# Dealing the projection units anew among the attention quarters, and multiplying by V four quarters at a time

## The chip, the core and the metric

The kernel runs on one core of a Trainium2 chip. The metric is the time of one launch on the device, in microseconds (us), as the median of several runs. Five engines work side by side: TensorE (PE in the profile; its weight loads are PEld), VectorE (DVE), ScalarE (ACT), GpSimd (POOL) and SyncE (SP), which here only issues DMAs.

## What is computed

One layer of an image backbone: 1024 latent tokens of 1024 numbers each, laid out as a grid of 16 rows by 64 columns, and 256 context tokens. Cut to what matters here (the norms, the modulation and the context's own projection are left out):

```python
q, k, v, za, u, bg, cg, zc = jnp.split(h @ w_in, SPLIT_POINTS, axis=-1)   # eight parts of 512 columns
# 8 heads of 64: softmax over a window of 8 x 16 latent keys (with a bias) and all 256 context keys
p = jax.nn.softmax(jnp.concatenate([s_lat, s_ctx], axis=-1), axis=-1)
o = p_lat @ v + p_ctx @ vc
attn = o * jax.nn.silu(za)
conv = bg * centred_short_conv(cg * u, conv_w, conv_b) * jax.nn.silu(zc)
x_new = x + gate[:, None] * (jnp.concatenate([attn, conv], axis=-1) @ w_out)
```

Everything is kept in 32-bit floats. A projection is done as three matmuls of split operands (high times high, high times low, low times high), so each weight tile is first cast into a high part on ACT (tile `uh`) and a low part on DVE (`ul`).

## The kernel before, in words

The program has four stages: the modulation and the norm, up to about 71 us; the projections to q, k and v (up to about 255 us); the attention; and the output projection.

**The attention stage is a loop over quarters.** A quarter is two blocks of 128 latent keys of one head, so a head has four and the loop `quarter(n)` has 32, and three more turns to drain. In this text a quarter's position is n modulo 4. In turn n, PE first transposes running maxima of quarter n-2 (`pmx<-ci,mx`, two small matmuls), then makes the scores of quarter n (`pss`) and the context scores of quarter n+1 (`pc`), and turns the reduced maxima back (`pmx<-ci,rm`). DVE reduces the maxima (`rm<-pmx`), adds up exponentials (`sum<-sum,sb`), adds the bias to the scores of quarter n (`sb<-pss,bt`), subtracts the maxima from quarter n-2 (`sc<-sc,mg` and `sb<-sb,mg`), and folds quarter n into the running maxima (`mx<-pc,sc`, then `mx<-mx,sb`). ACT copies, and takes the exponentials of quarter n-2. All four compute engines run in the order of the code (`strict`); SP's DMAs are not bound to it.

**Multiplying by V.** `weighted` (line 995) multiplies finished exponentials by V into the PSUM tile `po`. Its output is 64 columns wide, and the two halves of `po` (partitions 0 to 63 and 64 to 127) are fed in turn from two lists, sorted by size. Before, it is called in every second turn (o = n-3 even) with two quarters. `total` then sums the exponentials of a finished head (`pmx<-sum,onef`), and `finish` copies both out on ACT (`sums`, `ob`).

**Units and portions.** What is left of the input projection, 16 units of 128 columns, fills PE between these pieces (`unit`, line 369). A unit has two halves of 512 tokens, each with a PSUM bank of tile `pu` (two banks in all), and is cut into 8 portions of six matmuls, four to a half. `TICKS[n]` says how many portions turn n runs: one ahead of `weighted`, the rest behind it. Eight portions run ahead of the loop. Units come in three kinds: the gates of the attention, `attn_group(f)`, whose halves ACT copies to tile `z` and SP stores; and for each group i of the convolution `conv_group(i)`: U and C (tile `ub` on ACT, product `cu` on DVE), its gate z, and G. A convolution's gate keeps both banks until ACT has taken the SiLU of both halves (`zs<-pu`), which is queued when the unit ends and issued at the end of that turn. I write z0 to z3 for the gates of the attention, and U1, C1, zc1, G1 and so on for the groups.

**Chores.** What follows from a unit is queued (`chore`, line 325): ACT's share is issued at the end of the turn (`do_acts`), DVE's share near the start of the next one (`do_dves`), behind the sums and ahead of the bias. A group of the convolution gives DVE two products (`cu`), four taps (`cv<-cu,vecT,cv`), two products with the SiLU (`cv<-zs,cv`) and two with G (`cv<-pu,cv`); a unit gives two `ul`. When a pair of heads is done, `gated(f)` (line 1219 on) loads its row sums and its gate, takes a reciprocal, the SiLU of the gate (`held`, `silus`), and in two later turns multiplies (`zs<-zs,rb`, `tb<-tb,zs`). The exponential and the SiLU need different tables on ACT, so a SiLU costs an ACT_TABLE_LOAD ahead of it and one behind.

**The end.** After the loop the rest of zc3 and G3 runs, and the row sums of the last heads go out and back by DMA to a reciprocal on DVE (`recip`, line 521) that stands ahead of the last `ul` there.

Of the kernel before, what the change touches and what calls it, by code (L numbers as in the profile page):

```python
# [10 lines left out]
F32 = mybir.dt.float32  # L11
# [8 lines left out]
P = 128  # L20
# [7 lines left out]
NPAIR = NH // 2  # L28
# [1 line left out]
CTXT = 3  # L30
FORDER = [4, 5, 6, 0, 1, 2, 3, 7]

TICKS = [2, 3, 3, 3] + 2 * (3 * [4, 2] + [4, 3]) + 6 * [4, 2] + [5, 4, 4]
EPS = 1e-6

LOADS = "x0 x1 x2 x3 s0 c0 s1 c1 x4 x5 x6 x7 t10 t11 s2 t02 t12 c2"
# [19 lines left out]
def body(tc, es, x, xb, xt, cb_, ct, w_mod, w_gate, b_ada, w_grp, w_col, q_g, k_g, bias, w_out, vecs, cst, out):  # L56
# [451 lines left out]
    def attn_group(f):  # L508

        def keep(half, ps):  # L510
            z = cvp.tile([P, 512], F32, name="z", tag="ub", bufs=2)
            act.copy(z, ps)
            sp.dma_start(z_d[f][:, half * 512:(half + 1) * 512], z)

        for got in unit(z_col(f)):
            if got:
                chore(lambda got=got: keep(*got))
            else:
                yield
# [331 lines left out]
    class head:  # L851
# [30 lines left out]
        def ctx_scores(self, g, between=None):  # L882
            pc = psm.tile([P, 2, 256], F32, name="pc", tag="C", bufs=2)
            q = self.q[:, 1, g * 256:(g + 1) * 256]
            for i in range(2):
                if i and between:
                    between()
                for l in range(2):
                    pe.matmul(pc[:, i], self.kc[:, l, i * P:(i + 1) * P], q,
                              start=(i == 0 and l == 0), stop=(i == 1 and l == 1), skip_group_check=True)  # L890
            sc = ap.tile([P, 2, 256], F32, name="sc", tag="sc", bufs=6)
            act.copy(sc, pc)
            self.cps[g] = sc, pc

# [100 lines left out]
    def weighted(quarters):  # L995

        sides = [], []
        for m in quarters:
            for i, hd_, j in pair_of(m):
                if j == 0:  # L1000
                    hd_.po = psm.tile([P, 512], F32, name="po", tag="O", bufs=2)[:]
                for piece in hd_.pieces(j, sbs[m][:, i]):
                    sides[piece[0]].append((hd_, *piece))
            hd_ = heads[m // 4]
            for piece in hd_.ctx_pieces(m % 4):
                sides[piece[0]].append((hd_, *piece))
        for bank, side in enumerate(sides):
            side.sort(key=lambda piece: -piece[-1].free_size())
        for k in range(max(map(len, sides))):
            for bank, side in enumerate(sides):  # L1010
                if k < len(side):
                    hd_, _, j, dst, src = side[k]
                    pe.matmul(dst, hd_.v[:, j], src, start=k == 0 and (hd_, bank) not in opened, stop=k == len(side) - 1,
                              skip_group_check=True)
                    opened.add((hd_, bank))

# [2 lines left out]
    def quarter(n):  # L1019

        live = lambda m: 0 <= m < 4 * NH
        ticks = TICKS[n]
        e, o = n - 2, n - 3
        final = o == 4 * NH - 1
        left = do_frees(1) + 2 if n > 2 else 3
        if live(o):
            heads[o // 4].ctx_sum(o % 4)
        back = maxima(e) if e >= 0 else None
        for m in (o - 1, o)[:1 + final]:
            for i, hd_, j in pair_of(m):  # L1030
                hd_.lat_sum(j, sbs[m][:, i])
        do_dves(left)
        if gating and next(gating[0], "end"):
            gating.pop(0)
        now = pair_of(n)
        for i, hd_, j in now:
            hd_.scores(j, sbank[:, i])
        if n == 0:
            next(fill)
            ticks -= 1  # L1040
        ctx_now = [m for m in ([0, 1] if n == 0 else [n + 1]) if live(m)]
        for m in ctx_now:
            heads[m // 4].ctx_scores(m % 4, back if n >= 2 else None)
        if back and not ctx_now:
            if not now:
                next(fill, None)
                ticks -= 1
            back()

        def biased():  # L1050
            sb = sbs[n] = sb_new()
            bt = now[0][1].bt[:].rearrange("p v n -> p (v n)")[:, :1128].rearrange("p (a n) -> p a n", a=2)
            for at, slot, w_ in (((0, 31, 8), (8, 15, 16)), ((0, 0, 31),), ((0, 0, 31),), ((0, 0, 15), (15, 39, 8)))[n % 4]:
                dve.tensor_tensor(sb[:, :, at * 12:(at + w_) * 12], sbank[:, :, at * 12:(at + w_) * 12],
                                  bt[:, :, slot * 12:(slot + w_) * 12], ALU.add)

        if now and n >= 2:
            biased()
        if live(e):
            heads[e // 4].ctx_exp(e % 4)  # L1060
            w = both(sbs[e], e)
            w4 = w.rearrange("p a (c r) -> p a c r", r=12)
            dve.tensor_tensor(w4, w4, maxima_of(e), ALU.subtract)
            act.activation(w, w, AF.Exp)
        for _ in range(n > 0):
            next(fill, None)
        done = []
        if live(o) and (o % 2 == 0 or final):
            weighted([m for m in ((o - 1, o) if o % 2 == 0 else (o,)) if live(m)])
            if o % 4 == 0 and o or final:  # L1070
                hd_ = heads[(o - 1) // 4]
                pm = back_pm.pop() if not final else psm.tile([P, 512], F32, name="pmx", tag="C", bufs=2)
                hd_.total(pm)
                done.append((hd_, pm))
                if hd_.s:
                    ready.append(hd_.p)
        if now:
            if n < 2:
                biased()
            for m in ctx_now:  # L1080
                heads[m // 4].ctx_max(m % 4)
            for i, hd_, j in now:
                hd_.lat_max(j, sbs[n][:, i])
        back = maxima(-1) if n == 1 else None
        for _ in range(ticks - (n > 0)):
            next(fill, None)
        if back:
            back()
        for hd_, pm in done:
            hd_.finish(pm)  # L1090
        do_acts()
# [3 lines left out]


    def fillers():
        for unit_ in [attn_group(f) for f in range(NPAIR)] + [conv_group(i) for i in range(1, 4)]:
            for got in unit_:
                if got is None:  # L1100
                    yield

    units = [z_col(f) for f in range(NPAIR)]
    for i in range(1, 4):
        units += [CU + i * P, CCG + i * P, z_col(4 + i), CBG + i * P]
    follows.update(zip(units, units[1:]))
    fill = fillers()

# [110 lines left out]
    def gated(f):  # L1219
# [8 lines left out]
        dve.reciprocal(ri, ri)  # L1228
        sp.dma_start(ri_d[f].rearrange("h (x c) -> (h x) c", c=16), ri)
        held.append(zs)  # L1230
        if f:
            chore(lambda: silus(()))
        yield
        while held:
            yield
# [11 lines left out]
    with sbuf("att") as ap, psum("psb") as psb:  # L1247
        sbank = psb.tile([P, 2, 512], F32, name="pss")
        strict[:] = every
        mx = ap.tile([P, T], F32, name="mx")  # L1250
        sb_new = lambda: ap.tile([P, 2, 384], F32, name="sb", tag="sb", bufs=5)
        mg = ap.tile([P, T], F32, name="mg")
        heads[0].load_v()
        for n in range(len(TICKS)):
# [173 lines left out]
```

## Time and profile before

| | us |
|---|---|
| runs: median of three (lowest, highest) | 623.62 (622.5, 623.86) |
| the profiled execution | 622.72 |
| its span, first to last instruction | 620.9 |
| PE busy in the span | 599.6 (97%) |
| DVE, ACT, POOL busy | 399.0, 270.0, 66.9 |
| mean granted PE clock | 0.995 of full speed |

A row of a timeline reads: start, length, engine, line, operation, output <- input, shape, count, and in brackets the idle time of that engine just before and who ended it. Equal neighbours are merged into one row. Nearly every row has line 71, a helper that records operations, so rows are told apart by their tiles. Matmuls overlap, so a row's length is more than its share of the time; starts are the better measure. A row of windows gives, for a stretch that I chose, its length, then for PE, PEld, DVE, ACT and POOL the busy time and the number of instructions, then the granted PE clock, the DMA engines' busy share and GB/s.

### The profile page before, as it was taken

Reading aid. Unit: us, or ns where it says so; the run is one execution under the profiler, and the core shown is the slowest. Engines: PE = TensorE matmul, PEld = TensorE weight load, DVE = VectorE, ACT = ScalarE, POOL = GpSimd, SP = SyncE. Lnnn points to the kernel's source line nnn. Section 1 sums busy time; section 2 is a strip of 40 time slices with the busy share of each in tenths; the row PEclk is TensorE's granted clock in tenths of the full one; section 3 lists DMA queues with packets and bytes.
Section 4 is the critical chain, followed back from the end, with each engine's and each line's share of the span. In section 5 each row is a group of like instructions: output and inputs, shape, how many; then the busy total and the mean of one; then the engine's idle time right before and its main releaser. Section 6 shows DMA issues by size and latency. Waiting matters only on the chain.

```text
span 620.9 us, 9462 instructions
## 1 busy us (share of the span) xinstructions
PE 599.6 (97%) x3348; PEld 502.1 (81%) x3348; DVE 399.0 (64%) x833; ACT 270.0 (43%) x634; POOL 66.9 (11%) x86
## 2 busy tenths in 40 slices
PE   7799999999999999999999999999599999999998
PEld 3577899999999999878787877787378778887887
DVE  1567778556636456577787999879958756484211
ACT  5646354437436364344444373446345425451000
POOL 1001034023223222000000000000000002003300
PEclk9999999999999999999999999999989999999999
DMA  8995567534525674944536364828212316962731
GB/s 324 417 415 185 201 221 216 170 133 145 184 77 170 223 245 153 360 155 177 181 134 233 115 244 137 279 69 297 86 56 86 103 52 204 342 202 99 240 102 51
DMA packets 63226, 116.13 MB, mean 187 GB/s; under 512 B 7377, under 2 KB 26313, under 8 KB 60876
## 3 DMA queue, kind: packets, MB, share of 16 engines
q1 hardware_dynamic: 56684, 103.95, 48.1%
q10 hardware_dynamic: 6240, 11.05, 5.3%
q0 software_dynamic: 256, 0.54, 0.3%
q8 instruction: 26, 0.43, 0.3%
q14 instruction: 20, 0.16, 0.1%
HBM read 86.08 MB, written 29.43 MB: 186 GB/s over the span
## 4 chain that ended last, share of the span: by engine, by line
PE 80%; DVE 8%; DMA 6%; ACT 3%; issue 2%; ACTq 0%; SPq 0%; POOL 0%; DVEq 0%
PE pu L71 26%; PE pacc L71 21%; PE acc L71 5%; PE po L71 4%; PE cacc L71 4%; DMA woraw<-in_w_out 3%; PE pout L90 3%; PE pout L92 3%; PE pout L91 3%; DMA xn<-in_xb 3%; PE pmx L71 3%; PE pss L71 2%; PE pc L71 2%; DVE sb L71 1%; PE tr L71 1%
## 5 line engine op out<-in xcount | busy, mean ns | idle before, releaser
L71 PE MATMUL pu<-h,uh 128*128 128x512 f32 x544 | 172.8, 399 | 7.6 <-ACT zs L71 7.6
L71 PE MATMUL pacc<-w,h 128*128 128x384 f32 x768 | 138.9, 337 | 1.0 <-ACT ub L71 0.6
L71 PEld LDWEIGHTS pacc<-w,h 128*128 128x128 f32 x768 | 132.7, 188 | 1.9 <-ACT ub L71 1.0
L71 PEld LDWEIGHTS pu<-h,uh 128*128 128x128 f32 x544 | 98.9, 190 | 30.8 <-ACT zs L71 8.2
L71 PE MATMUL pu<-h,ul 128*128 128x512 f32 x272 | 107.1, 394 | 0.0
L71 PEld LDWEIGHTS pu<-h,ul 128*128 128x128 f32 x272 | 51.5, 189 | 11.4
L71 POOL TENSOR_TENSOR ss<-ss,few 128x4 f32<-128x4 f32 (+1 forms) x40 | 41.8, 1046 | 125.7 <-DVE ss L71 125.3
L90 PE MATMUL pout<-woh,yh 128*128 128x512 f32 (+2 forms) x136 | 51.6, 380 | 0.1
L91 PE MATMUL pout<-wol,yh 128*128 128x512 f32 (+2 forms) x136 | 51.6, 379 | 0.0
L92 PE MATMUL pout<-woh,yl 128*128 128x512 f32 (+2 forms) x136 | 51.0, 380 | 0.0
L71 ACT ACTIVATE sc<-sc 128x512 f32<-128x512 f32 x32 | 20.2, 632 | 54.4 <-DVE sc L71 54.4
L71 ACT COPY mg<-pmx 128x256 f32<-128x256 f32 (+1 forms) x33 | 12.1, 367 | 66.2 <-PE pmx L71 64.7
L71 DVE TENSOR_REDUCE rm<-pmx 128x2 f32<-128x256 f32 (+1 forms) x33 | 13.7, 416 | 40.3 <-PE pmx L71 40.3
L71 PE MATMUL acc<-h,w 128*128 128x512 f32 x144 | 37.2, 403 | 1.2 <-ACT h L71 1.2
L71 DVE TENSOR_REDUCE ss<-sq 128x4 f32<-128x260 f32 (+1 forms) x40 | 15.7, 393 | 28.6 <-ACT sq L71 27.7
L71 PEld LDWEIGHTS acc<-h,w 128*128 128x128 f32 x144 | 25.8, 188 | 9.3 <-ACT h L71 2.0
L71 DVE TENSOR_TENSOR mx<-mx,sb 128x372 f32<-128x372 f32 (+2 forms) x64 | 31.9, 498 | 1.9
L71 ACT ACTIVATE sq<-pacc 128x256 f32<-128x256 f32 x32 | 12.4, 387 | 47.2 <-PE pacc L71 46.5
L71 DVE TENSOR_TENSOR sum<-sum,sb 128x372 f32<-128x372 f32 (+2 forms) x64 | 31.6, 494 | 1.2
L71 ACT ACTIVATE qn<-pacc,ss 128x64 f32<-128x64 f32 x128 | 30.1, 330 | 4.9 <-PE trA L71 2.5
L90 PEld LDWEIGHTS pout<-woh,yh 128*128 128x128 f32 x136 | 25.6, 188 | 5.3 <-ACT yh L1319 0.6
L92 PEld LDWEIGHTS pout<-woh,yl 128*128 128x128 f32 x136 | 25.6, 188 | 4.8 <-DVE yl L1320 0.2
(141 smaller groups left out, 949.7 us busy)
## 6 DMA issues: line engine op xcount, KB each, us to landing
uraw<-in_w_col SPq DMA_DIRECT2D x34, 256.0 KB
slab<-in_w_mod SPq DMA_DIRECT2D x8, 1024.0 KB
q_d<-qs SPq DMA_DIRECT2D x32, 256.0 KB
k_s<-k_d SPq DMA_DIRECT2D x8, 1024.0 KB
q_s<-q_d SPq DMA_DIRECT2D x16, 512.0 KB
wr<-in_w_grp SPq DMA_DIRECT2D x40, 192.0 KB
bt<-in_rpb SPq DMA_DIRECT2D x8, 564.0 KB
xn<-in_xb SPq DMA_DIRECT2D x8, 512.0 KB
```

Source lines behind the costliest of these rows:

```text
L71: i = emit(*a, **kw)
L90: i = pe.matmul(ps, ah, bh, start=first, stop=False)
L91: pe.matmul(ps, ah, bl, start=False, stop=False)
L92: pe.matmul(ps, al, bh, start=False, stop=last)
```

## The change

Four things. `TICKS` is new: portions still sum to 110 over the 35 turns. The units stand in another order: z0, U1, C1, zc1, G1, z1, U2, C2, zc2, G2, z2, z3, U3, C3, zc3, G3, where before all of z0 to z3 came first. `weighted` is called in every fourth turn with four quarters (and at the end with three), and a first matmul into a bank is now found by the set `opened` alone; two rings of tiles grow from 6 to 8 and from 5 to 7 for it. And the SiLU of the first pair's gate has its own chore, where before it went with that of zc1.

```diff
-TICKS = [2, 3, 3, 3] + 2 * (3 * [4, 2] + [4, 3]) + 6 * [4, 2] + [5, 4, 4]
+TICKS = [2, 3, 3, 3] + 3 * [4, 4, 4, 1] + [4, 4, 4, 2] + 2 * [4, 4, 3, 1] + [4, 4, 2, 1] + [4, 4, 3]
...
-            sc = ap.tile([P, 2, 256], F32, name="sc", tag="sc", bufs=6)
+            sc = ap.tile([P, 2, 256], F32, name="sc", tag="sc", bufs=8)
...
-                    pe.matmul(dst, hd_.v[:, j], src, start=k == 0 and (hd_, bank) not in opened, stop=k == len(side) - 1,
+                    pe.matmul(dst, hd_.v[:, j], src, start=(hd_, bank) not in opened, stop=k == len(side) - 1,
...
-        if live(o) and (o % 2 == 0 or final):
-            weighted([m for m in ((o - 1, o) if o % 2 == 0 else (o,)) if live(m)])
+        if live(o) and (o % 4 == 0 or final):
+            weighted([m for m in range(o - 2 - (o % 4 == 0), o + 1) if live(m)])
...
-        for unit_ in [attn_group(f) for f in range(NPAIR)] + [conv_group(i) for i in range(1, 4)]:
+        for unit_ in (attn_group(0), conv_group(1), attn_group(1), conv_group(2), attn_group(2), attn_group(3), conv_group(3)):
...
-    units = [z_col(f) for f in range(NPAIR)]
+    units = [z_col(0)]
     for i in range(1, 4):
-        units += [CU + i * P, CCG + i * P, z_col(4 + i), CBG + i * P]
+        units += [CU + i * P, CCG + i * P, z_col(4 + i), CBG + i * P] + [z_col(f) for f in ((1,), (2, 3), ())[i - 1]]
...
-        if f:
-            chore(lambda: silus(()))
+        chore(lambda: silus(()))
...
-        sb_new = lambda: ap.tile([P, 2, 384], F32, name="sb", tag="sb", bufs=5)
+        sb_new = lambda: ap.tile([P, 2, 384], F32, name="sb", tag="sb", bufs=7)
```

The portions by turn, counted off the two tables (a unit has portions 0 to 7): before, turn 26 runs zc2.7, G2.0, G2.1, G2.2, so a convolution's gate ends inside a turn. In the changed kernel, turn 7 runs zc1.7 alone (ahead of `weighted`) and turn 8 G1.0 to G1.3; turn 19 runs zc2.6 and zc2.7 and turn 20 G2.0 to G2.3. The ends of C1, C2, zc1, G1, zc2 and G2 lie in turns 5, 17, 7, 9, 19 and 21; they lay in 12, 23, 15, 18, 26 and 28.

On ACT, before, the SiLU of zc2 (turn 26) stands behind that turn's exponentials (`sc`, `sb`) and a table load:

```order
L71 COPY mg<-pmx 128x256
L71 COPY sc<-pc 128x512
L71 ACTIVATE sc<-sc 128x512
L71 ACTIVATE sb<-sb 128x2x288
L71 ACT_TABLE_LOAD
L71 ACTIVATE zs<-pu 128x512 x2
```

In the changed kernel, on ACT at the first such place (zc1, turn 7), the row sums and the output of a head are copied (`sums`, `ob`) between the exponentials and the SiLU:

```order
L71 ACTIVATE sc<-sc 128x512
L71 ACTIVATE sb<-sb 128x2x372
L71 COPY sums<-pmx 128x256
L71 COPY ob<-po 128x512
L71 ACT_TABLE_LOAD
L71 ACTIVATE zs<-pu 128x512 x2
```

So the SiLU on which G waits has moved behind copies that themselves wait for the group by V.

On PE, before, a group of two quarters of one head (turn 5; the tile `v_3052` is V of that head) stands between portions:

```order
L71 MATMUL po<-sb,v_3052 64x23x12
L71 MATMUL po<-sb,v_3052 64x24x12
L71 MATMUL po<-sb,v_3052 64x23x12
L71 MATMUL po<-sb,v_3052 64x24x12
L71 MATMUL po<-sc,v_3052 64x256 x4
L71 MATMUL po<-sb,v_3052 64x7x12
L71 MATMUL po<-sb,v_3052 64x8x12
L71 MATMUL po<-sb,v_3052 64x7x12
L71 MATMUL po<-sb,v_3052 64x8x12
L71 MATMUL pu<-h_164,uh 128x512 x2
```

In the changed kernel, on PE in turn 7, the group of four quarters (three of the first head, V in `v_3055`, and one of the next, `v_3056`) begins so:

```order
L71 MATMUL po<-sb,v_3056 64x24x12
L71 MATMUL po<-sb,v_3055 64x24x12
L71 MATMUL po<-sb,v_3056 64x24x12
L71 MATMUL po<-sb,v_3055 64x24x12
L71 MATMUL po<-sb,v_3055 64x23x12 x4
L71 MATMUL po<-sc,v_3055 64x256 x4
L71 MATMUL po<-sc,v_3056 64x256
```

Pieces of 24 x 12 columns now stand beside pieces of 24 x 12, and those of 23 x 12 beside their like.

On DVE, before, turn 17 holds one `ul` and the two products of `gated` between the sums and the bias:

```order
L71 TENSOR_REDUCE rm<-pmx 128x2
L71 TENSOR_TENSOR sum<-sum,sb 128x31x12 x2
L71 TENSOR_TENSOR ul<-uraw,uh 128x512
L71 TENSOR_TENSOR zs<-zs,rb 128x512
L71 TENSOR_TENSOR tb<-tb,zs 128x512
L71 TENSOR_TENSOR sb<-pss,bt 128x2x372
```

In the changed kernel, turn 17 on DVE holds five chores there:

```order
L71 TENSOR_REDUCE rm<-pmx 128x2
L71 TENSOR_TENSOR sum<-sum,sb 128x31x12 x2
L71 TENSOR_TENSOR ul<-uraw,uh 128x512
L71 TENSOR_TENSOR cu<-pu,ub 128x2x16x16
L71 TENSOR_TENSOR ul<-uraw,uh 128x512
L71 TENSOR_TENSOR zs<-zs,rb 128x512
L71 TENSOR_TENSOR tb<-tb,zs 128x512
L71 TENSOR_TENSOR sb<-pss,bt 128x2x372
```

A second `ul` and a product `cu` came to it, since C2 now ends in this turn.

## The prediction

> **What bounds the kernel now.** I read the page first, then the list of waits, then windows cut at the start of each turn of the attention loop, and last the timelines at the turns that are too long.
>
> ```profile
> span 620.9 us, 9462 instructions
> PE   7799999999999999999999999999599999999998
> PE pu L71 <- ACT zs L71: 7.6, 2, 7.0
> 365.85:373.70 7.85, 7.24 (x38) 6.01 (x37) 6.74 (x14) 7.60 (x12) 0.13 (x2) 1.00 0.80 324
> 373.70:381.95 8.25, 7.27 (x50) 5.40 (x48) 7.92 (x15) 2.67 (x5) 0.00 (x0) 1.00 0.47 156
> ...
> 425.20:432.50 7.30, 7.09 (x37) 5.82 (x37) 6.90 (x15) 3.22 (x7) 0.00 (x0) 1.00 0.98 377
> 432.50:440.19 7.69, 7.09 (x49) 5.41 (x49) 7.29 (x14) 4.04 (x7) 0.00 (x0) 1.00 0.40 135
> 440.19:456.30 16.11, 9.16 (x36) 7.33 (x37) 8.79 (x16) 4.54 (x7) 0.13 (x2) 0.79 0.15 49
> 456.30:463.27 6.97, 6.97 (x49) 4.86 (x48) 6.48 (x14) 4.70 (x8) 0.00 (x0) 1.00 0.13 30
> 463.27:470.20 6.93, 6.93 (x37) 5.91 (x36) 6.43 (x14) 3.02 (x6) 0.00 (x0) 1.00 0.54 173
> 470.20:477.10 6.90, 6.90 (x49) 5.48 (x48) 5.98 (x12) 3.68 (x6) 0.00 (x0) 1.00 0.28 86
> 477.10:484.15 7.05, 7.05 (x37) 6.05 (x36) 5.30 (x10) 5.78 (x10) 0.00 (x0) 1.00 0.08 28
> 484.15:491.49 7.34, 6.85 (x45) 4.27 (x44) 6.82 (x14) 1.96 (x4) 0.00 (x0) 1.00 0.42 142
> 491.49:511.06 19.57, 19.57 (x107) 14.49 (x107) 11.95 (x23) 5.54 (x11) 0.00 (x0) 1.00 0.22 69
> 511.06:528.89 17.83, 17.83 (x82) 14.75 (x79) 10.52 (x17) 10.08 (x16) 3.40 (x6) 1.00 0.67 202
> ```
>
> PE is full but for one slice, the 29th. The windows are turns 16, 17, 24 to 31 and the drain, each from PE's first matmul on the maxima to the next. Where PE is busy for the whole window (27 to 30) I read what a turn needs of PE: position 0 (four portions) 6.93, position 1 (two portions and a group of two quarters) 6.90, position 2 (four portions) 7.05, position 3 (two portions, a group of two and the row sums) 6.97. Against these, turn 16 loses 0.92, turn 17 1.35, turn 24 0.37, turn 25 0.79, turn 26 9.06 and turn 31 0.37: 12.86 us in all, and that is nearly all that can be won from waits. The last window holds 13 portions, so a portion is 17.83 / 13 = 1.37 us.
>
> Turn 26 shows what its 9 us are:
>
> ```profile
> 447.01 0.63 ACT L71 ACTIVATE sc<-sc 128x512 f32<-128x512 f32 x1 [4.38 <-DVE sc L71]
> 448.37 1.28 ACT L71 ACT_TABLE_LOAD   x1
> 450.31 1.22 PE L71 MATMUL pu<-h,uh 128*128 128x512 f32 x2 [6.95 <-ACT zs L71]
> ```
>
> The first portion of the turn ends zc2, G2 wants a bank at once, and both banks wait for a SiLU that ACT issues only behind that turn's exponentials, which wait for DVE. PE stands for 6.95 us, and the window's mean clock is 0.79, so the rest of the 9.06 is matmuls at a lower clock. A wait of 2.36 us early in the program,
>
> ```profile
> 24.95 0.65 PE L71 MATMUL tr<-ci,sums 128*128 128x128 f32 x4 [2.36 <-POOL sums L71]
> ```
>
> left no such mark, so waits of up to that length I count without a loss of clock.
>
> The shorter losses come from DVE. Turn 25:
>
> ```profile
> 426.85 0.69 DVE L71 TENSOR_TENSOR cu<-pu,ub 128x512 f32<-128x512 f32 x1
> 428.78 0.81 DVE L71 TENSOR_TENSOR sb<-pss,bt 128x192 f32<-128x192 f32 x2
> 432.95 0.42 DVE L71 TENSOR_REDUCE rm<-pmx 128x2 f32<-128x256 f32 x1 [0.26 <-PE pmx L71]
> 434.32 0.69 DVE L71 TENSOR_TENSOR ul<-uraw,uh 128x512 fp32r<-128x512 f32 x1
> 434.93 1.53 DVE L71 SCALAR_TENSOR_TENSOR cv<-cu,vecT,cv 128x512 f32<-128x512 f32 x2
> 436.38 0.93 DVE L71 TENSOR_TENSOR sb<-pss,bt 128x744 f32<-128x744 f32 x1
> 438.91 1.13 DVE L71 TENSOR_TENSOR mx<-mx,sb 128x372 f32<-128x372 f32 x2
> 457.90 1.29 DVE L71 TENSOR_TENSOR cv<-zs,cv 128x512 f32<-128x512 f32 x2
> ```
>
> DVE's first step (`rm`) needs this turn's transposes on PE, and PE's next transposes need DVE's last step (`mx`). So a turn lasts as long as the longer of the two, and the loop holds no credit from one turn to the next. From start to start, an `ul` takes 0.61 and two taps 1.45, so turn 25 without chores would be 7.69 - 2.06 = 5.63 on DVE; I take that for positions 1 and 2. Turn 24 (position 0) held one product `cu`, one `zs` and one `tb`, 1.93 in all (426.85 to 428.78): 7.30 - 1.93 = 5.37 for position 0. Of the 1.93 I give 0.60 to `cu`, 1.33 to the pair. Two products with the SiLU are 1.2, as the row of 1.29 less the overlap. A test on turn 17 (an `ul`, the pair, and a product with G ahead of its reduce, of which 0.54 counts): 5.63 + 0.61 + 1.33 + 0.54 = 8.11, measured 8.25.
>
> **The change part by part.** *Turn 26 and the old DVE losses.* All six turns get other chores or other portions: -12.86.
>
> *Groups of four.* A group's body between two portions, from the rows
>
> ```profile
> 435.61 1.19 PE L71 MATMUL po<-sb,v 128*64 128x276 f32 x8
> 437.93 0.73 PE L71 MATMUL pu<-h,uh 128*128 128x512 f32 x2
> ```
>
> is 2.32 us. A merged position 3 then needs 6.97 - 1.37 + 2.32 = 7.92 (one portion), and position 1, with four portions and no group, 7.05 as position 2 does: 14.97 with five portions, 13.60 with four, against 6.90 + 6.97 = 13.87. So a merged group saves 0.27, seven times by turn 31: -1.89. [...]
>
> *Portions.* TICKS has two more portions up to turn 31 and two fewer behind: +2.74 here, taken back below.
>
> *DVE's new places.* Need of PE: position 0 6.93, positions 1 and 2 7.05 with four portions, 5.68 with three, 4.31 with two. Only turns that DVE or a bank lengthens are listed:
> - 5: two `ul`, one `cu`: 5.63 + 1.82 = 7.45, +0.40.
> - 9: one `ul`, two products with the SiLU: 7.44, +0.39.
> - 10: a product with G ahead of the reduce (0.54), another (0.60), an `ul`: 7.38, +0.33.
> - 17: two `ul`, `cu`, the pair of `gated`: 5.63 + 3.15 = 8.78, +1.73.
> - 20: three taps (2.18): 7.55, +0.62. Turn 8 has the same, below.
> - 21: `ul`, two products, a reciprocal (0.2): 7.64, +0.59.
> - 22: as 10, against three portions: 7.38 - 5.68 = +1.70.
> - 25: `ul` and a pair: 7.57, +0.52.
> - 26: an `ul`, three portions: 6.24 - 5.68 = +0.56.
> - 30: an `ul`, two portions: 6.24 - 4.31 = +1.93.
>
> *The SiLU at turns 7 and 8.* What a SiLU behind `finish` costs is in turn 15:
>
> ```profile
> 365.31 0.36 ACT L71 COPY sums<-pmx 128x256 f32<-128x256 f32 x1
> 366.17 1.28 ACT L71 ACT_TABLE_LOAD   x1
> 368.11 0.74 PE L71 MATMUL pu<-h,uh 128*128 128x512 f32 x2 [0.61 <-ACT zs L71]
> 464.73 0.62 PE L71 MATMUL pu<-h,uh 128*128 128x512 f32 x2
> ```
>
> From the copy of the sums to PE's next portion it is 368.11 - 365.31 = 2.80. In turn 7 no portion stands behind the group, so the copy starts about as turn 8 does; PE wants the bank 464.73 - 463.27 = 1.46 into a turn. With 0.1 for the hand-over that is a wait of 1.4, in place of the 9 of turn 26. The three taps of turn 8 (0.62 too long) hide under it: +1.4. In turns 19 and 20 a portion (1.37) stands behind the group, 1.37 + 1.46 = 2.83 against 2.9: nothing, but with no cover left; if ACT is 1 us late there, it costs 1. ACT's own SiLU for the first pair adds two table loads in turns 13 and 14; ACT was busy 3 to 4 us of most turns above, and DVE's chores lie ahead of the step that waits for ACT: 0, at most 2 x 1.28 if that cover is gone.
>
> The sum of new losses is 0.40 + 1.4 + 0.39 + 0.33 + 1.73 + 0.62 + 0.59 + 1.70 + 0.52 + 0.56 + 1.93 = 10.17.
>
> *Loads and stores on SP.* Each unit's two weight loads, and the gates' stores, move with the units past the loads of q, k and V on SP. In turns 8, 10, 20, 25 and 28 a unit's load and its cast now fall into one turn. The shortest distance that I found before was
>
> ```profile
> 465.60 0.33 SPq L319 DMA_DIRECT2D uraw<-in_w_col  x1
> 468.51 0.60 ACT L71 CAST uh<-uraw 128x512 fp32r<-128x512 f32 x1
> ```
>
> 2.9 us with no wait; a turn is 7, so 0 (a rival below). POOL's two small memsets of `cu` move with the groups; POOL is idle there: 0. The larger rings cost no time.
>
> *The end.* From turn 32 to the row sums of the last head, one portion fewer (-1.37) and one group instead of two (-0.27, with like beside like -0.3): -1.67. The second portion that left, behind the sums, I count at nothing:
>
> ```profile
> 517.09 0.25 DVE L71 RECIPROCAL ri<-ri 128x16 f32<-128x16 f32 x1 [8.98 <-DMA ri<-rs_d]
> 517.26 1.23 DVE L71 TENSOR_TENSOR ul<-uraw,uh 128x512 fp32r<-128x512 f32 x2
> ```
>
> DVE's last reciprocal ends a round trip of DMAs that begins with PE's last row sums (511.06), and G3's first `ul` stands behind it, ready 517.26 + 0.61 = 517.87, 6.8 us after the sums. Before, five portions (6.85) covered that to the hair; now four (5.48) do, and PE waits the 1.37 that it was to save.
>
> **Sum:** -12.86 + 10.17 + 2.74 - 1.89 - 1.67 = -3.5 us. On the profiled execution, 622.72, that is 619.2. The median of the three runs (623.62) is 0.9 above that execution and its lowest run 0.2 below, so I leave the forecast at 619.2. Two tenths of a per cent, which a measurement of this kernel can just tell from no change, is 1.25 us.
>
> **The rivals.**
>
> *DVE's turns are shorter than I reckon.* If half of the 10.17 shows (chores that fill gaps in which DVE waits for PE or ACT anyway), it is 619.2 - 5.1 = 614.1. For it: in turn 25 DVE is busy 7.29 of 7.69. Against it: turn 17 came out longer than reckoned.
>
> [...]
>
> *A switch of the table costs twice its row.* If ACT must also run empty ahead of a load, a SiLU comes 1.28 later, at turn 8 and, with the cover gone, at turn 20: 619.2 + 2.6 = 621.8. Against it: the 2.80 of turn 15 hold two copies, the load's 1.28 and the SiLU, and leave no room for it. [...]
>
> *Slower: weights that come late.* SP is one queue, in which a load can be held behind a store that waits for DVE. In the five turns named, a load issued later than 7.0 - 2.9 = 4.1 us into the turn makes ACT wait in its cast, and behind it stand the next turn's copy of the maxima and exponentials, on which DVE and then PE wait. If each is held to the sixth microsecond, that is 5 x 2 = 10 us: 629; from about 1 us each it is slower than before. Against it: the buffers come free by the `ul` of the turn before or early in the same one.
>
> **How the numbers follow.** The forecast (619.2, on its own 617 to 621.5, from the errors of the DVE terms and of turn 20) 0.66; half of the DVE losses 0.12; no gain from groups 0.08; dearer switches 0.07; late weights 0.07. The range reaches to the first rival at 614.5, and to 622.0 on the other side, past the second and third; it leaves out late weights and a little on each side. Faster by over 1.25: the forecast, the first rival and most of the second, less the forecast's upper tail, 0.80; within: the third, the rest of the second and that tail, 0.12; slower: 0.08.
>
> **What would show it.** Right: no wait of PE for `zs` over 2 us and no slice below 0.9 of the clock in the attention; PE's wait for `zs` near 1.4 once, at turn 8; turns 17, 22 and 30 losing 1.5 to 2 us each, with DVE busy throughout; merged turns of 7.9; a wait of PE for DVE's `ul` of about 1.4 just behind the last row sums. Wrong: a wait for `zs` at turn 20, ACT waiting for a DMA of `uraw`, or turns 5 to 26 at PE's own length.

## The result, and the profile after

| | before | after |
|---|---|---|
| median of 20 runs (lowest, highest), us | 623.27 (621.29, 624.61) | 620.88 (617.75, 624.9) |
| the profiled execution | 622.72 | 620.61 |
| its span | 620.9 | 618.7 |
| PE busy in the span | 599.6 | 597.5 |

The ratio of the runs is 0.996, with an interval of 0.9946 to 0.9973. The change wins 2.4 us on the medians and 2.1 between the two profiled executions; 3.5 was forecast. Two rows of the page's slices, and then, from the list of PE's waits, those in the loop and behind it (in all, times, longest, us), of the changed kernel:

```profile
PE   7899999999999999999999998999999899999998
PEclk9799999999999999999999999999999999999999
```

```profile
PE pmx L71 <- DVE mx L71: 5.5, 7, 1.7
...
PE pmx L71 <- ACT uh L71: 1.9, 2, 1.6
...
PE pout L90 <- ACT yh L1318: 1.4, 1, 1.4
PE pu L71 <- ACT zs L71: 1.3, 1, 1.3
PE pu L71 <- DVE cu L71: 1.2, 1, 1.2
```

The slice with the 7 us wait is gone, and no wait for `zs` is above 1.3. In its place stand many shorter waits, and a lower clock in the second slice, far ahead of the attention. The windows of turns 5, 7, 8, 16, 17, 22 and 30:

```profile
288.76:296.17 7.41, 7.33 (x37) 5.87 (x36) 6.89 (x13) 2.17 (x4) 0.00 (x0) 1.00 0.23 73
303.25:310.82 7.57, 7.57 (x67) 5.17 (x66) 6.71 (x14) 3.06 (x6) 0.00 (x0) 1.00 0.65 205
310.82:319.34 8.52, 7.21 (x40) 6.01 (x37) 7.09 (x14) 7.24 (x11) 0.13 (x2) 1.00 0.68 266
...
370.19:378.93 8.74, 7.14 (x41) 5.84 (x37) 4.91 (x11) 3.79 (x8) 0.00 (x0) 1.00 0.93 340
378.93:387.69 8.76, 7.27 (x36) 5.97 (x37) 8.37 (x16) 2.58 (x5) 0.00 (x0) 1.00 0.38 123
418.94:426.04 7.10, 5.94 (x30) 4.85 (x31) 7.00 (x14) 5.38 (x9) 0.00 (x0) 1.00 0.52 166
...
476.09:482.32 6.23, 4.51 (x26) 3.70 (x24) 5.71 (x11) 5.09 (x9) 0.00 (x0) 1.00 0.19 70
```

Turns 17 and 22 have DVE busy nearly throughout (8.37 of 8.76, 7.00 of 7.10) and PE not, and turn 30 has DVE at 5.71 and PE at 4.51 of 6.23: they are DVE's turns, as forecast. The merged turn 7 is all PE's, at 7.57. Turn 16 is neither's: PE 7.14 and DVE 4.91 of 8.74. Something else holds it. Coarser windows, of after and then of before (the loop from turn 2 to 31; turn 32 to the last row sums; from there to the output projection; that to the end):

```profile
268.38:489.68 221.30, 212.50 (x1267) 168.57 (x1265) 185.15 (x367) 112.04 (x192) 0.27 (x4) 1.00 0.48 161
489.68:508.45 18.77, 17.56 (x96) 13.56 (x93) 11.76 (x22) 5.29 (x10) 0.00 (x0) 1.00 0.22 71
508.45:525.50 17.05, 17.05 (x82) 13.72 (x81) 9.22 (x15) 9.36 (x15) 3.40 (x6) 1.00 0.63 171
525.50:618.70 93.20, 88.92 (x409) 74.26 (x407) 36.01 (x57) 16.71 (x29) 10.24 (x8) 0.99 0.52 175
```

```profile
267.34:491.49 224.15, 214.30 (x1254) 169.27 (x1253) 184.93 (x367) 108.53 (x190) 0.26 (x4) 0.98 0.46 159
491.49:510.49 19.00, 19.00 (x98) 14.33 (x99) 11.95 (x23) 5.54 (x11) 0.00 (x0) 1.00 0.23 71
510.49:528.89 18.40, 18.40 (x87) 14.91 (x87) 10.52 (x17) 10.08 (x16) 3.40 (x6) 1.00 0.65 196
528.89:620.90 92.01, 88.97 (x409) 74.26 (x407) 34.76 (x55) 16.02 (x27) 10.23 (x8) 1.00 0.50 170
```

So the 2.1 between the two executions is made up of +1.04 ahead of turn 2 (268.38 against 267.34), -2.85 in the loop, -0.23, -1.35, +1.19, and +0.09 outside the span (1.91 against 1.82).

### The profile page after: what moved, and what is told of

Its sections match the earlier page's. It is cut to its first block, busy times and chain, and to the rows that moved or that the text cites. A ratio compares the mean times of both kernels' runs of the same rounds, so it can differ in the third digit from the quotient of the medians.

```text
span 618.7 us, 9470 instructions
## 1 busy us (share of the span) xinstructions
PE 597.5 (97%) x3347; PEld 501.0 (81%) x3348; DVE 399.4 (65%) x833; ACT 273.4 (44%) x636; POOL 66.4 (11%) x86
## 4 chain that ended last, share of the span: by engine, by line
PE 75%; DVE 10%; DMA 10%; ACT 2%; issue 2%; ACTq 1%; SPq 1%; DVEq 0%
PE pacc L71 21%; PE pu L71 20%; PE acc L71 5%; PE po L71 4%; PE pout L92 4%; PE pout L90 4%; PE pout L91 4%; PE cacc L71 4%; DMA slab<-in_w_mod 3%; PE pmx L71 3%; DVE sb L71 2%; PE pss L71 2%; DVE mx L71 2%; DMA tb<-y_d 2%; DMA woraw<-in_w_out 2%
## 5 line engine op out<-in xcount | busy, mean ns | idle before, releaser
L71 PE MATMUL pu<-h,uh 128*128 128x512 f32 x544 | 169.6, 393 | 2.6 <-ACT zs L71 1.3
L71 PE MATMUL acc<-h,w 128*128 128x512 f32 x144 | 38.5, 413 | 0.0
```

The lines of the kernel that those rows point to most:

```text
L71: i = emit(*a, **kw)
```

## The experiments

Each ratio is to runs of the kernel before on the same chip; their medians were 623.5 (e1 to e4), 624.28 (e5 to e8) and 624.31 (e9 to e11).

| kernel | median us (lowest, highest) | ratio to before |
|---|---|---|
| e1_before_shift | 618.49 (616.3, 618.99) | 0.9906 (0.9886 to 0.9926) |
| e2_pairs | 623.1 (620.43, 625.19) | 0.9988 (0.9972 to 1.0005) |
| e3_pool_stores | 618.08 (616.06, 621.42) | 0.9916 (0.9886 to 0.9946) |
| e4_retimed | 619.34 (617.47, 623.21) | 0.9933 (0.9906 to 0.9959) |
| e5_retimed_stores | 613.48 (613.11, 614.48) | 0.9829 (0.9797 to 0.9861) |
| e6_less_g3 | 618.62 (617.09, 621.65) | 0.9922 (0.9893 to 0.9951) |
| e7_sp_loads | 620.77 (618.55, 1934.78) | 0.9947 (0.9927 to 0.9968) |
| e8_two_calls | 622.33 (620.2, 624.34) | 0.9968 (0.9947 to 0.9989) |
| e9_end_table | 612.74 (610.57, 615.56) | 0.9816 (0.9787 to 0.9845) |
| e10_old_units | 616.83 (615.99, 618.6) | 0.9885 (0.9861 to 0.9909) |
| e11_rb_pool | 618.14 (617.31, 619.48) | 0.9908 (0.9882 to 0.9933) |

**Is the new deal needed to lose the 9 us?** One number of the old table moved:

```diff
-TICKS = [2, 3, 3, 3] + 2 * (3 * [4, 2] + [4, 3]) + 6 * [4, 2] + [5, 4, 4]
+TICKS = [2, 3, 3, 3] + 2 * (3 * [4, 2] + [4, 3]) + 2 * [4, 2] + [4, 3, 3, 2] + 2 * [4, 2] + [5, 4, 4]
```

> The kernel before with one number of TICKS moved: turn 25 runs three portions and turn 26 three, so zc2 ends with turn 25 and G2 begins with turn 26. Theory (the 9.06 us of turn 26 come only from a gate that ends in mid-turn, and a turn lasts as long as the longer of PE and DVE): turn 25 becomes 6.90 + 1.37 = 8.27 by PE, turn 26 becomes 5.63 + 0.61 + 1.45 + 1.33 = 9.0 by DVE's chores in place of 16.1, no wait of PE for zs over 1 us, in all -6.5: 616.5 on the profiled execution of the kernel before, which is faster than the changed kernel (620.6). Rival (the order of the units and the groups of four are what wins the turn back; G2 waits for the SiLU wherever the gate ends): a wait of 5 us or more stays in turn 26, and the time is 621 or more.

Measured: 618.49, 2.4 below the changed kernel's median; the intervals of the two ratios do not meet. Its turns 25, 26 and 27:

```profile
434.08:442.36 8.28, 8.28 (x54) 6.64 (x55) 7.47 (x14) 5.06 (x8) 0.00 (x0) 1.00 0.43 141
442.36:451.44 9.08, 5.87 (x32) 4.83 (x30) 8.42 (x15) 4.81 (x8) 0.13 (x2) 1.00 0.25 88
451.44:459.97 8.53, 8.53 (x49) 6.34 (x50) 6.83 (x15) 3.78 (x7) 0.00 (x0) 0.80 0.09 32
```

Turns 25 and 26 are as reckoned (8.27, 9.0), its longest wait for `zs` in the loop is 0.6, and the rival is out: it was the place of a gate's end in its turn. Turn 27 was not foreseen: PE is busy for all of it, at a clock of 0.80, after DVE had kept PE waiting for 3.2 us (its wait for `mx`) in turn 26. That took back 8.53 - 6.97 = 1.6.

**What a merged group saves.** First the changed kernel with groups of two:

```diff
-TICKS = [2, 3, 3, 3] + 3 * [4, 4, 4, 1] + [4, 4, 4, 2] + 2 * [4, 4, 3, 1] + [4, 4, 2, 1] + [4, 4, 3]
+TICKS = [2, 3, 3, 3] + 3 * [4, 2, 4, 3] + [4, 2, 4, 4] + 2 * [4, 2, 3, 3] + [4, 2, 2, 3] + [4, 4, 3]
-        if live(o) and (o % 4 == 0 or final):
-            weighted([m for m in range(o - 2 - (o % 4 == 0), o + 1) if live(m)])
+        if live(o) and (o % 2 == 0 or final):
+            weighted([m for m in ((o - 1, o) if o % 2 == 0 else (o,)) if live(m)])
```

> The changed kernel with groups of two quarters in positions 1 and 3 again, and with two portions moved from position 1 to position 3 of each four turns, so that each four turns hold the same portions. Theory (a merged group saves 7.92 - 7.57 = 0.35 more than the 0.27 I forecast, so 0.62 for each of the seven): PE needs 4.3 more by turn 31; DVE's losses in the loop are by the same reckoning 1.8 smaller than in the changed kernel: +2.5, 623.1. Rival (a merged group saves 0.27 as forecast, and the turns of 7.57 are short for another reason): +1.9 - 1.8 = 0.1, 620.7. In the trace the turns of position 1 that no chore of DVE lengthens (13, 29) should be near 6.9.

Measured: 623.1. Its turns 13 and 27, bounded by PE alone:

```profile
349.41:356.33 6.92, 6.92 (x50) 5.50 (x49) 5.98 (x12) 3.69 (x6) 0.00 (x0) 1.00 0.27 87
...
456.96:465.31 8.35, 8.35 (x55) 5.99 (x55) 5.53 (x13) 3.70 (x7) 0.00 (x0) 1.00 0.39 119
```

Five portions and two groups of two take 6.92 + 8.35 = 15.27; the same five and a merged group take 7.07 (turn 13 of the changed kernel, between its starts at 348.48 and 355.55) + 7.57 = 14.64. A merged group saves 0.63. The second kernel asks whether that is the switches between a portion's 128 columns and a group's 64 or the pairing of pieces:

```diff
-            weighted([m for m in range(o - 2 - (o % 4 == 0), o + 1) if live(m)])
+            ms = [m for m in range(o - 2 - (o % 4 == 0), o + 1) if live(m)]
+            for two in (ms[:-2], ms[-2:]):
+                if two:
+                    weighted(two)
```

> The changed kernel with the same multiplications by V in position 3, but as two lists of two quarters, one right behind the other with no portion between: the pieces pair up as in the kernel before, the number of switches between 128 and 64 columns is that of the changed kernel. Theory (a merged group saves 0.6 because two switches are gone): merged turns stay at 7.6, 620.9 in all. Rival (it saves because pieces of like size stand beside each other): the merged turns are 0.5 longer, near 8.1, +3.5 in all, 624.4.

Measured: 622.33, but the total misleads here. Its turn 7:

```profile
304.57:312.14 7.57, 7.57 (x67) 5.61 (x65) 6.71 (x14) 3.06 (x6) 0.00 (x0) 1.00 0.63 206
```

The merged turn is 7.57, so pairing of like sizes is out. What is left of the two explanations is the switches; that a switch costs time is not shown, since no kernel varied them by themselves. The profiled execution is 2.0 longer than the changed kernel's: its turn 2 starts 1.3 later, and turn 16 is 9.77 in place of 8.74, for the reason that comes next.

**Turn 16.** The timeline of the changed kernel: ACT in that turn, SP's load of K ahead of it, and what DVE then waits for. Behind it the page's row on such loads, with the KB of each and the us to landing:

```profile
370.33 0.37 ACT L71 COPY sums<-pmx 128x256 f32<-128x256 f32 x1 [1.09 <-PE pmx L71]
...
373.41 0.51 ACTq L946 DMA_DIRECT2D rs_d<-sums  x1
374.32 1.10 ACTq L951 DMA_DIRECT2D o_d<-ob  x2
375.52 0.37 ACT L71 COPY mg<-pmx 128x256 f32<-128x256 f32 x1 [4.33 <-DMA rb<-ri_d]
364.83 0.62 SPq L862 DMA_DIRECT2D k_s<-k_d  x1
375.93 0.69 DVE L71 TENSOR_TENSOR sc<-sc,mg 128x512 f32<-128x512 f32 x1 [3.24 <-ACT mg L71]
```

```profile
k_s<-k_d SPq DMA_DIRECT2D x8, 1024.0 KB, 8.2
```

The row sums are copied by 370.70, but their store is issued at 373.41, and ACT's copy of the maxima, which stands behind it, comes 5.3 into the turn. DVE waits for that, and PE's next transposes wait for DVE's last step and for a cast of ACT's (`uh`) behind the same hold; the two end within 0.1 us of each other. The compiled program's waits say why: each DMA of SP and ACT uses one of eight semaphores in turn, and its issue waits for the DMA that used it last. These are the rows of K's load, eight DMAs later the store of the sums, and the two stores of the output:

```
L862 DMA k_s<-k_d_85 128x1x2048 [waits DMAHW6_49]
...
L946 DMA rs_d_72<-sums 4x256 [waits DMAHW6_49,Activation_49]
L951 DMA o_d_58<-ob 64x512 [waits DMAHW7_49,Activation_49]
L951 DMA o_d_58<-ob 64x512 [waits DMAHW0_49]
```

K's load of 1 MB was issued at 364.83; the trace has the last update of its semaphore at 373.33, and the store of the sums is issued at 373.41. The two stores of the output follow the loads that had their semaphores in the same way: `uraw` (landed 374.25, store issued 374.32) and `rb` (374.80 and 374.82). So the row of the copy names `rb`, the last that ACT waited for. First, the stores off ACT:

```diff
+            queue = pool if self.p < NPAIR - 1 else act
...
-            act.dma_start(rs_d[self.p][self.s].rearrange("b (x c) -> (b x) c", c=256),
+            queue.dma_start(rs_d[self.p][self.s].rearrange("b (x c) -> (b x) c", c=256),
...
-                act.dma_start(o_d[self.p][64 * self.s:64 * self.s + 64, bank * 512:(bank + 1) * 512], ob[64 * bank:64 * bank + 64])
+                queue.dma_start(o_d[self.p][64 * self.s:64 * self.s + 64, bank * 512:(bank + 1) * 512], ob[64 * bank:64 * bank + 64])
```

> The changed kernel with the three stores behind a finished head (row sums and both halves of the output) issued by POOL in place of ACT, for the heads of the first three pairs; the last pair's stay on ACT. Theory (turn 16 is 1.8 too long because ACT stood in the issue of the row sums' store until a load of rb had landed, and its copy of the maxima stood behind it): turn 16 is 6.95 in place of 8.74, ACT's copy of the maxima comes about 1.3 into the turn and not 5.3, in all -1.8: 618.8. Rival (ACT or DVE is late in turn 16 because of weights uraw or because the DMA engines are full of k and q): turn 16 stays at 8.5 or more, 620.6.

Measured: 618.08, turn 16 at 6.97 with the DMA engines fuller than in the changed kernel (share 1.00 against 0.93):

```profile
369.23:376.20 6.97, 6.97 (x40) 5.95 (x37) 5.01 (x11) 4.21 (x8) 1.69 (x3) 1.00 1.00 358
```

My expectation had named `rb`; the second kernel tells the semaphore from crowding:

```diff
-            load_sums(f, half, rb, sp)
+            load_sums(f, half, rb, pool)
```

> The changed kernel with the loads of rb (128 KB each) issued by POOL in place of SP, for the first three pairs. In the list of waits each DMA of SP and ACT takes one of eight semaphores in turn, and waits for the DMA that had it before: in turn 16 of the changed kernel the store of the row sums has that of the 1 MB load of K (issued at 364.83, such a load lands after 8.2), the first store of the output that of uraw, the second that of rb. With rb gone from the row the store of the sums has that of a load of q, and only the second store of the output that of K. Theory (ACT is held by the semaphore of K): the store of the sums is issued 0.5 after its copy and not 2.7, the last store is held until about 8.5 after K's issue, ACT's copy of the maxima comes 1.0 to 1.5 earlier, turn 16 is 7.2 to 7.7 in place of 8.74, 619.5. Rival (the store is held because the DMA engines are full): the store of the sums still waits 2 us or more, turn 16 stays at 8.7, 620.9.

Measured: 618.14. ACT in turn 16:

```profile
369.03 0.37 ACT L71 COPY sums<-pmx 128x256 f32<-128x256 f32 x1 [1.11 <-PE pmx L71]
...
369.43 0.51 ACTq L946 DMA_DIRECT2D rs_d<-sums  x1
370.04 3.64 ACTq L951 DMA_DIRECT2D o_d<-ob  x2
373.78 0.37 ACT L71 COPY mg<-pmx 128x256 f32<-128x256 f32 x1 [3.89 <-PE pu L71]
```

The store of the sums now goes out at once, and the hold has moved to the last store, the one that shares K's semaphore: K's load is issued at 363.50 and lands at 373.21, and that store is issued at 373.23. That shows the cause. The size was missed: the copy comes 4.75 after that of the sums, not 5.19, and turn 16 is 8.29, above the 7.2 to 7.7 expected. The hold had been reckoned to end 8.5 after K's issue, and here K took 9.7. That its median is 2.7 below the changed kernel's is more than this: its profiled execution gains 0.43 in the loop, 1.35 ahead of it (below) and 0.5 at the end.

**Portions dealt by the rule of the longer engine.**

```diff
-TICKS = [2, 3, 3, 3] + 3 * [4, 4, 4, 1] + [4, 4, 4, 2] + 2 * [4, 4, 3, 1] + [4, 4, 2, 1] + [4, 4, 3]
+TICKS = [2, 3, 4, 3] + 2 * [4, 4, 4, 1] + [4, 3, 4, 1] + [3, 5, 4, 2] + [4, 4, 4, 1] + [3, 4, 3, 1] + [3, 3, 4, 1] + [4, 4, 3]
```

> The changed kernel with another TICKS alone (99 portions up to turn 31 as before): portions go to turns 2, 17, 22 and 30 and leave 13, 16, 19 by one more order, 24, 28 and 29, so that turns with many chores of DVE have more of PE's work and zc1 ends with turn 6. Theory (a turn lasts as long as the longer of PE and DVE, with the prices of the prediction, 7.57 for a merged turn): the losses of turns 5, 8 to 10, 17, 22 and 30 fall from 8 us to about 1, -6.9 in the loop, 613.7 if turn 16's wait of ACT stays or goes with the new order of DMAs by no more than 1.8. Rival (portions that are moved make new waits on banks, on the SiLU or on late weights, so that such a table wins nothing): 618 or more, with waits of PE over 1 us for zs, uh or cu.

Measured: 619.34, so the theory failed as it stood. Its turns 16 and 17:

```profile
368.68:378.77 10.09, 5.77 (x34) 4.74 (x31) 4.91 (x11) 3.69 (x7) 0.00 (x0) 0.91 0.87 311
378.77:389.56 10.79, 10.79 (x43) 9.29 (x44) 7.95 (x15) 2.77 (x5) 0.00 (x0) 0.76 0.22 73
```

In turn 16 the store of the sums is issued at 372.86, 9.5 after K's load (8.6 in the changed kernel). The hold ends with K's landing (372.79), whatever PE has to do; that is 4.1 into the turn, where it was 3.1 in the changed kernel (and 4.1 in e8, whose turn 16 is 1.0 longer). With one portion fewer to cover it PE waits 4.3, and then turn 17 runs at 0.76 of the clock. Turn 24 is held by the next load of K in the same way (landed 440.15, store issued 440.23): it is 9.37, with a wait of 3.6, and turn 25 runs at 0.81. Both edits together (those of e3 and e4):

> The table of e4 and POOL's stores of e3 together. Theory (e4 lost its gain to ACT standing in the issue of the row sums' stores in turns 16 and 24, and to the lower clock in the turn behind each wait of 3.6 and 4.3): turn 16 falls from 10.09 to 5.6, turn 17 from 10.79 to 8.5, turn 24 from 9.37 to 5.6, turn 25 from 8.57 to 7.6, in all 11.5 off e4's loop of 225.75: 214.2, no wait of PE over 1.3 us in the loop, 611 to 613. Rival (the moved portions bring other waits, such as weights late on SP): a loop of 219 or more, 617.

Measured: 613.48. Its turns 16 and 17:

```profile
368.08:373.69 5.61, 5.61 (x34) 4.82 (x31) 5.01 (x11) 3.69 (x7) 1.69 (x3) 1.00 1.02 350
373.69:383.06 9.37, 8.58 (x43) 7.06 (x42) 7.57 (x14) 2.67 (x5) 0.00 (x0) 1.00 0.59 214
```

Turns 16 and 24 are 5.6 as reckoned; 17 and 25 (9.37 and 8.32) are 0.9 and 0.7 longer than reckoned. In both, DVE stands idle ahead of its second product of the pair, 1.27 and 0.82, for a load on SP (`tb<-o_d`, issued at 374.44 and 434.87, landed at 378.57 and 439.07; the product starts 0.08 behind each landing). In turn 17:

```profile
378.65 0.69 DVE L71 TENSOR_TENSOR tb<-tb,zs 128x512 f32<-128x512 f32 x1 [1.27 <-issue]
```

What makes that load late is open. In e9 below, with the same numbers up to turn 31, turn 17 is 8.52, as reckoned, and turn 25 is 9.68, with DVE idle there for 2.18. By the medians the two edits together win 7.4 against the changed kernel, where e4 alone won 1.5 and e3 alone 2.8: e4's gain was behind the hold. With the old order of the units (z0 to z3 first), e3's edit and this table:

```diff
+TICKS = [2, 3, 4, 2] + [3, 4, 4, 1] + [4, 3, 6, 1] + [3, 4, 4, 2] + [4, 5, 3, 1] + [3, 3, 4, 2] + [5, 5, 4, 1] + [2, 3, 3, 1] + [4, 4, 3]
```

> The kernel of e5 with the units in the order of before (z0 to z3 first) and a table of its own that follows the same rules: each convolution's gate ends with its turn, and turns with many chores of DVE have more portions. Theory (where a gate ends against its turn, and how portions lie against DVE's chores, decides; the order of the units only sets what must lie where): the same reckoning gives a loop 1.1 longer than for e5's table, 614.5, at most 616. Rival (that gate units stand between the groups is what counts, because it spreads DVE's chores): 618 or more.

Measured: 616.83, between the two expectations. It meets a wait of 2.2 for `cv` in turn 26 that the reckoning lacked, and turn 27 behind it runs at 0.83 of the clock:

```profile
452.41:461.37 8.96, 8.96 (x67) 6.53 (x65) 4.94 (x11) 2.42 (x4) 0.00 (x0) 0.83 0.15 50
```

The old order gets to 0.9885 of before, the new one to 0.9829. So the old order, with a new table and POOL's stores, wins more than the whole change did (0.996). How much of the rest belongs to the order isn't shown: part of it is that wait and the lower clock behind it, and I tried one table for the old order.

**The end.** Three portions of G3 left out:

```diff
-                mm3(ps, *w[k], hh[k][:, cols], hl[k][:, cols], k == 0, k == KT - 1)
+                if col != CBG + 3 * P or not half or k < 2:
+                    mm3(ps, *w[k], hh[k][:, cols], hl[k][:, cols], k == 0, k == (1 if col == CBG + 3 * P and half else KT - 1))
```

> The changed kernel with three of the twelve portions behind the last row sums left out (those of the last half of G3, which then sums over a quarter of its inputs): 4.1 us less work for PE at the end. Theory (the output projection is held by its transfers, whose start is set by ACT's SiLU of zc3 and not by PE's end, so what PE gains ahead of it comes back as waits for yh or weights): PE reaches the output projection 4.1 earlier, its waits there grow from 1.4 to about 5, and the time changes by less than 1: 620 to 621. Rival (the output projection is bound by PE, and the 1.4 is an accident): 616.8, with waits there still near 1.4.

Measured: 618.62. The output projection, from its first matmul to the end:

```profile
521.11:615.20 94.09, 89.52 (x409) 74.29 (x408) 37.98 (x60) 18.41 (x31) 10.25 (x8) 1.00 0.54 185
```

PE arrives 13.11 after the sums and not 17.05, 3.94 earlier, and the output projection is 94.09 long against 93.20: 0.9 comes back, not 4.1, and PE's longest wait for `yh` there is still 1.4, so my theory falls. The ten profiles besides this one, the changed kernel's and e7's have 91.45 to 93.39 there, so up to 2.6 may have come back. The loads of the output projection by SP:

```diff
-                sp.dma_start(y_d[4 + i][:, half * 512:(half + 1) * 512], cvs[half])
+                (pool if i == 3 else sp).dma_start(y_d[4 + i][:, half * 512:(half + 1) * 512], cvs[half])
...
-        act.dma_start(raw, w_out[0, f * P:(f + 1) * P, nh * 512:(nh + 1) * 512])
+        sp.dma_start(raw, w_out[0, f * P:(f + 1) * P, nh * 512:(nh + 1) * 512])
...
-                act.dma_start(zs, z_d[f][:, cols])
-                act.dma_start(tb, o_d[f][:, cols])
+                sp.dma_start(zs, z_d[f][:, cols])
+                sp.dma_start(tb, o_d[f][:, cols])
...
-                act.dma_start(tb, y_d[f][:, cols])
+                sp.dma_start(tb, y_d[f][:, cols])
```

> The changed kernel with the loads of the output projection (weights and y) issued by SP in place of ACT, and the two stores of the third convolution group by POOL so that SP is free. Theory (the output projection waits because ACT issues its loads behind its own work and waits): the first loads start about 4 us earlier, near 510 us and not 514.8, the wait for yh of 1.4 goes, -1.4: 619.5. Rival (the transfers themselves bound that stretch, or the loads wait for the buffers of the attention to come free): the first loads start at 514 or later, or the wait of 1.4 stays: 620.9.

Measured: 620.77, nothing won. Its one profile is of an execution of 1934.78 us, in which matmuls took two to nearly three times as long from end to end, so where the loads begin otherwise isn't known, and this one tells little. Last, the end of e5's table:

```diff
-... + [3, 3, 4, 1] + [4, 4, 3]
+... + [3, 3, 4, 1] + [3, 4, 4]
```

> The kernel of e5 with the last three numbers of TICKS 3, 4, 4 in place of 4, 4, 3: C3's last two portions run in turn 33 ahead of zc3's first, and no portion is added or left out ahead of the row sums. Theory (PE's 1.21 for cu in turn 33 is there because zc3 wants the bank of C3's first half one portion too early for DVE's product): the wait goes, the row sums come 1.2 earlier after turn 32's start (17.6 for 18.8), 612.3. Rival (the end is held by something else, the product comes later as well, or PE's portions meet another wait of this size): 613.5.

Measured: 612.74; the intervals of e9 and e5 overlap, so the total shows no gain by itself. Turn 32 to the sums, and from there to the output projection:

```profile
485.72:501.93 16.21, 16.20 (x91) 12.37 (x87) 11.68 (x22) 5.19 (x10) 0.00 (x0) 1.00 0.26 81
501.93:520.31 18.38, 18.38 (x87) 14.90 (x87) 10.33 (x17) 10.67 (x17) 3.21 (x6) 1.00 0.67 188
```

The wait for `cu` is gone. My expectation had one thing wrong: the edit also moves a portion from ahead of the sums to behind them. Together the two stretches are 34.59 against 35.81 in e5 and 18.77 + 17.05 = 35.82 in the changed kernel: 1.2 won, the wait's own size. The profiled execution is the slowest of the six all the same (615.56): PE waits 2.45 at the end of its turn 25, and turn 26 behind it is 7.33 at 0.77 of the clock, against 6.26 in e5.

## Why the prediction was right, and where it was off

The time fell inside the range and on the side forecast, and the main mechanism held. That the 3.5 came out as near as 2.1 is in part luck, since errors cancel. Against the forecast, DVE's turns came to -0.5, the groups -2.4, turn 16 +1.8, the stretch up to the sums +1.4, that behind them -1.35, the output projection +1.2, and what lies ahead of the loop +1.0; with 0.2 of rests that is the 1.4.

**Right: old losses and DVE's turns.** What held the six old turns is gone, turn 26 above all (16.11 before, 6.25 now); turn 16 has a new loss in its place (below). Of the losses forecast, turn 5 is 7.41 (7.45 forecast), 17 is 8.76 (8.78), 26 is 6.25 (6.24), 30 is 6.23 (6.24); turn 22 is 7.10 (7.38). The wait for the SiLU at turn 8 is 1.3 (1.4), and there is none at turn 20. At both places ACT's table load of 1.28 begins 0.02 behind the copy ahead of it, and the SiLU 0.01 behind the load (311.82, 311.84 and 313.13 at turn 8; 403.38, 403.40 and 404.69 at turn 20). The list of turns comes to 9.65 for 10.17. This puts out the rivals of half the DVE losses and of the dearer table switch. The same rule held in e1; in e5 it missed turns 17 and 25, as said.

**Wrong size: groups.** The step "a merged position 3 then needs 6.97 - 1.37 + 2.32 = 7.92" took the body of four quarters as two bodies of 2.32. The group by V in turn 15 of the changed kernel, up to the row sums:

```profile
365.52 2.12 PE L71 MATMUL po<-sb,v 128*64 128x288 f32 x16
...
369.62 0.64 PE L71 MATMUL pmx<-sum,onef 128*32 128x256 f32 x8
```

It is 369.62 - 365.52 = 4.10 long, not 4.64. The seven merged turns together are 2.44 shorter than forecast; that groups bring no gain (0.08 in the prediction) is out by e2, where a merged group saves 0.63 and not the 0.27 forecast.

**Wrong: "Loads and stores on SP ... 0".** I followed SP past the weights and never ACT's own stores. In turn 16 ACT is held at one of them by a semaphore that a load of K has, +1.81 (e3, e11). The late weights of the rival did not occur: no wait of ACT for `uraw` is in the list of the loop.

**Wrong: the end.** -1.67 to the sums became -0.23: zc3 wants C3's bank before DVE's product, a wait of 1.21 (e9). I had looked at banks only for the SiLU. Behind the sums I counted 0 and 1.35 was won, since the round trip, from PE's last sums (at 508.45) to DVE's reciprocal, was shorter:

```profile
513.83 0.25 DVE L71 RECIPROCAL ri<-ri 128x16 f32<-128x16 f32 x1 [8.85 <-DMA ri<-rs_d]
```

5.38 from start to start, 517.09 - 510.49 = 6.60 before, so the wait of about 1.4 for `ul` that the prediction looked for there is not in the list. The three profiles with five portions behind the sums (before, e1, e9) have 6.6 to 6.7, the other nine 5.1 to 5.5. In those three ACT issues two loads of `y` within 0.5 us of the load of the sums (`ri<-rs_d`), which takes 3.2 to 3.4 to land; in the others the loads of `y` come about 3 us later, and it takes 1.8 to 2.2. That the loads of `y` stretch it is likely, but no kernel moved them by themselves. The output projection was 1.19 longer; it holds a wait for `yh` of 1.37 that other profiles with about the same 17.05 ahead of it have at 0 (e8), 0.3 (e5) and 0.7 (e3), so I take it for scatter.

**Wrong: "waits of up to that length I count without a loss of clock".** The same early wait of 2.36 is in the changed kernel, and here it left a mark. The row of the timeline, and then the window from 15.5 to 36 us, of the changed kernel and of the kernel before:

```profile
24.12 1.11 PE L71 MATMUL tr<-ci,sums 128*128 128x128 f32 x4 [2.36 <-POOL sums L71]
```

```profile
15.50:36.00 20.50, 17.84 (x106) 11.95 (x105) 10.37 (x20) 11.44 (x21) 1.01 (x1) 0.83 1.02 411
```

```profile
15.50:36.00 20.50, 16.94 (x114) 11.50 (x112) 12.19 (x27) 11.61 (x21) 1.01 (x1) 1.00 1.03 416
```

That is the +1.04 ahead of the loop, in code that the change does not touch. Of the twelve profiles (all but e7's) four have 1.00 in this window, and their turn 2 starts at 267.0 to 267.4; four have 0.92 (267.8 to 268.5), and four, the changed kernel's among them, 0.83 (268.4 to 269.7). What decides it is at the end of this document.

## What to carry to other kernels

Where two engines hand a loop's turn to each other, reckon each turn as the longer of the two and put movable work where the other engine is long: one portion moved (e1) won more than the whole change. Before moving work, list for each engine every DMA that it issues and which earlier DMA's end the issue waits for; such a hold ended 0.02 to 0.08 us behind that earlier DMA's landing in the six read here, and with less work to cover it the wait was longer (turn 16: 4.3 in e4 against 2.65 in e8, with the hold ending 4.1 into the turn in both). Judge an edit by its own turn in the trace when the total scatters by 1 to 2 us with a wait elsewhere (e8, e11).

## What the hardware showed that I had not expected

Waits of PE of 1.6 and 1.72 in the attention left the clock at 1.00; of 1.87 (e6, turn 16), 2.17 (e10), 2.45 (e9), 2.65 (e8), 3.2 (e1), 3.6 and 4.3 (e4) were each followed by a turn with a mean of 0.76 to 0.83. Early in the program 2.36 did it in some executions and not in others.

In the traces the falls lie on steps of one length. Wherever the clock falls in the twelve profiles, it goes to 0.50, and ahead of the last few us it stays there for one or two steps of 3.41 us. Where it falls more than once in a profile, the starts lie whole steps of 3.413 apart: in e4 they are at 11.79, 25.44, 377.01 and 445.28, which is 4, 103 and 20 steps. Cut along these steps, the early wait of 2.36 (21.77 to 24.12 in the changed kernel, 22.59 to 24.95 before) reads, first in the changed kernel and then before:

```profile
20.32:23.73 3.41, 1.45 (x7) 0.85 (x5) 0.17 (x1) 2.39 (x5) 0.67 (x1) 1.00 0.99 384
23.73:27.14 3.41, 2.72 (x20) 1.40 (x20) 1.25 (x2) 1.04 (x2) 0.34 (x1) 0.50 1.06 430
```

```profile
20.64:24.06 3.42, 1.95 (x9) 1.27 (x7) 0.46 (x2) 2.90 (x6) 0.17 (x1) 1.00 1.02 407
24.06:27.47 3.41, 1.68 (x20) 0.90 (x20) 1.21 (x2) 1.01 (x2) 0.84 (x1) 1.00 1.05 427
```

In the changed kernel PE has no work for 1.96 of the first step (3.41 - 1.45), and the next runs at half the clock; before, an edge splits the wait, and neither step has more than 1.73 without work. Between 15 us and the output projection, in all twelve profiles, every step at full clock in which PE had no work for 1.87 or more was followed by 0.50, and none with 1.76 or less was. So somewhat over half of a step without work was enough here (1.87 of 3.41). By these figures a wait from about 1.8 to an estimated 3.5 us (2 x 1.76, when an edge halves it) can cost clock in one execution and not in the next.
